# Half of the down projections' width as seven half-size products, and layer 1's attention on one folded block of keys

## The chip, the cores and the metric

The kernel runs on one core of a Trainium2 chip. The core has a matrix engine (PE, whose weight loads are listed as PEld), a vector engine (DVE), a scalar engine (ACT), a general engine (POOL), and a queue of its own for most DMA transfers (SP). They work beside each other and wait for each other through semaphores. SBUF is the core's working memory with 128 partitions; PSUM is the small memory that PE writes its sums to.

The metric is the time of one execution in microseconds, as the device measures it; the figure for a kernel is the median of several runs.

## The reference

One sequence of 512 tokens of width 1024 passes two layers. Layer 0 mixes the tokens with a gated delta rule, layer 1 with attention over a sliding window of 128 tokens; both add attention into 256 memory tokens, and both are followed by an MLP with 4096 hidden features.

```python
def sliding_window_sink_attention(q, k, v, sinks):
    ...
    s = jnp.einsum('bnqhgd,bnkhd->bnhgqk', qb, kk).astype(jnp.float32) * (dh ** -0.5)
    qi = jnp.arange(WINDOW)[:, None]
    kj = jnp.arange(2 * WINDOW)[None, :]
    diff = qi + WINDOW - kj
    band = (diff >= 0) & (diff < WINDOW)
    ...
    m = jnp.maximum(jnp.max(s, axis=-1, keepdims=True), sink)
    p = jnp.exp(s - m)
    denom = jnp.sum(p, axis=-1, keepdims=True) + jnp.exp(sink - m)
    probs = (p / denom).astype(v.dtype)
    o = jnp.einsum('bnhgqk,bnkhd->bnqhgd', probs, vv)

def sq_relu_mlp(h, w_up, w_down):
    return jnp.square(jax.nn.relu(h @ w_up)) @ w_down

    for layer in range(DEPTH):
        ...
        h = layer_norm(DN_ALPHA * h + mix, ln_g[layer, 0], ln_b[layer, 0])
        h = layer_norm(DN_ALPHA * h + sq_relu_mlp(h, mlp_w_up[layer], mlp_w_down[layer]),
                       ln_g[layer, 1], ln_b[layer, 1])
        if layer == N_A - 1:
            k_sh, v_sh = shared_kv(h, w_kv_shared, cos, sin)
```

With blocks of 128 tokens, a query sees key j of its own block where j is not after it, and key j of the block before where j is after it: for each j exactly one of the two.

## The kernel before

**Numbers.** Every large product is done with operands split in two: a high part, rounded to the form that PE multiplies quickly (float32r), and a low part, the rest. A product is three matmuls: high by high, high by low, low by high. `split` (L967) and `wload` (L102) make such a pair of tiles from a raw one (`wr`): ACT copies the high part (`wh`), DVE subtracts it from the raw tile (`wl`). `hidden` (L979) does the same to the hidden values after squaring them.

**The MLP** (`mlp`, L960 to L1233) goes through eight chunks of 512 hidden features. In one turn of the loop at L1198 the downs of chunk c stand beside the ups of chunk c + 1, in two sections, n = 0 and 1; with chunk 7 only downs are left (`downs_last`, L1157).

A section begins with the up products of a `Pair` (L1073): two blocks of 128 features, computed as a 2 x 2 block product with seven half-size products in place of eight, in the order m1, m6, m2, m7, m5, m4, m3. Each is 12 matmuls of 256 columns. The sums of tokens that this needs are made once per layer (`x_sums`). The sums of weights are made by POOL in `up_load` (L1052: four operations, from the raw tiles into `sa` and `sb`) and then split (`split0`, `split_b`, `split_a`, `split2`). The partial results are joined by DVE in `u2`, `u3` and the four quarters of `r`, which read PSUM; `close` applies ReLU and the square and splits the result.

Then come the downs of the section (`down`, L1138): for each of the four tiles of 128 tokens, twelve matmuls of 512 columns into one bank of PSUM (`mmt`, three banks in turn), which DVE adds to `res` (L1149). The weights are two slabs per section, by `dn_slab` (L1151). Between the four tiles the splits of the next section's pair are issued, so that they stand on ACT and DVE while PE works on the downs.

**Order.** PE's order is that of the program (`T`, a wrapper, chains each matmul to the one before where it matters). On the other engines the framework's scheduler may reorder; `behind(a, b)` puts a behind b without a wait. The gain and shift of the first layer norm are loaded by `load_gb` (L861) into a pool of their own before the MLP; those of the second at the end of chunk 1.

**Layer 1's mixer** runs the steps of LAYER1_ORDER (L41): w loads weights, k makes the shared keys and values, q the queries, a one `attend` (half of the heads, one tile of tokens), o an output projection, l a layer norm, and F empties the pipeline of units. `attend` pushes two units of four heads each. A unit has three stages, which are put between the other steps: `scores` (six matmuls per pair of heads over one or two blocks of keys; masked maximum by L1344; exponential by L1351; sink; scaling by L1362), `turn` (transposes of each 128 x 128 block of weights by PE into `spt`, copies to `pT`), and `values` (`ov`). Tile 0 has one block of keys, tiles 1 to 3 two. In half 1 the second unit is the memory's.

Of the kernel before, what the change touches and what calls it, by code (L numbers as in the profile page):

```python
# [18 lines left out]
P = 128  # L19
# [21 lines left out]
LAYER1_ORDER = """w2 k1 k2 w01 k0 k3 q11 q12 q10 a11 w00 q13 a10 q00 a13 a12 a00 q02 w10 q01 a01 a02 q03 w11 o00 a03 o01 F o02 o03  # L41
o11 o10 l1 o12 l0 o13 l2 l3"""
# [8 lines left out]
def trunk(ctx: ExitStack, tc: tile.TileContext, xT, xn, memT, wk, wq, wv, wqm, wz, wmk, wmv, wo0, wo1, up, dn,  # L51
# [38 lines left out]
    def mmt(n="mm"):  # L90
        return pmm.tile([P, 512], F32, tag="mm", name=nm(n))
# [769 lines left out]
    def load_gb(i):  # L861
        g_t = late[0].tile([P, D], F32, tag="lng", name=nm("lng"), bufs=1)
        b_t = late[0].tile([P, D], F32, tag="lnb", name=nm("lnb"), bufs=1)
        SY.dma_start(g_t, lng[i:i + 1, :].broadcast_to([P, D]))
        SY.dma_start(b_t, lnb[i:i + 1, :].broadcast_to([P, D]))
        return g_t, b_t
# [59 lines left out]
    gb0 = load_gb(0)  # L926
# [34 lines left out]
    def mlp(pool, layer, last, gb0):  # L961
# [5 lines left out]
        def f4(shape, n):  # L967
            return pool.tile(shape, F32, tag="f4", name=nm(n), bufs=5)
# [42 lines left out]
        def ups_second(hid):  # L1011

            for f in range(2):
# [3 lines left out]
                r = f4([P, 512], "relu")  # L1017
# [8 lines left out]
        def x_sums():  # L1026
# [5 lines left out]
            else:  # L1032
                f11, f12, f21, f22 = t1, *(f4([P, 4, HT], n) for n in ("f12", "f21", "f22"))
# [19 lines left out]
        def up_load(f, e):  # L1053
# [7 lines left out]
            e.tensor_tensor(sb[:, 1], raw[0][:, kB], sb[:, 0], op=ALU.subtract)  # L1061
            return raw, sa, sb
# [9 lines left out]
        class Pair:  # L1072


            def __init__(self, f0, e=G):
                self.f0 = f0
                self.raw, self.sa, self.sb = up_load(f0, e)

            def split0(self, first):
                hi, lo = split(self.raw[0], [P, KT, P], first=first)  # L1080
                self.A11, self.A12 = (hi[:, kA], lo[:, kA]), (hi[:, kB], lo[:, kB])

            def split_b(self):
                hi, lo = split(self.sb, [P, 2, 4, P])
                self.S2, self.S4 = ((hi[:, i], lo[:, i]) for i in range(2))

            def split_a(self, first=None):
                hi, lo = split(self.sa, [P, 2, 4, P], first=first)
                self.S1, self.S3 = ((hi[:, i], lo[:, i]) for i in range(2))

            def split2(self, first_act=None):
                self.A22 = split(self.raw[1][:, kB], [P, 4, P], "w2h", first_act=first_act)
# [16 lines left out]
            def m2(self):  # L1109
                product(self.a, self.A12, xq["B21"], False, True)  # L1110
                self.r = f4([P, 2, 512], "r")
                A.activation(self.r[:, 0, tA], self.a, AF.Relu)
# [11 lines left out]
            def m4(self):  # L1124
                product(self.b, self.A22, xq["T4"], False, True)
                V.tensor_tensor(self.r[:, 1, tA], self.s1, self.b, op=ALU.add)
# [29 lines left out]

        def downs_last(hid):  # L1157
# [27 lines left out]

        hid, nxt = ups_first()
        gb1 = done = None
        tables = rotary_tables(pool) if layer == 0 else None
        for c in range(NC - 1):
            later = new_hid()  # L1190
            for n in range(2):
                p, nxt = nxt, None
                f0 = 4 * c + 2 * n + 6
                early = c == n == 0
                if p is None:
                    ups_second(later)
                    slabs = dn_slabs(c, n)
                else:  # L1198
# [8 lines left out]
                    p.split2(None if early else done)  # L1207
                    slabs = [dn_slab(c, n, 0, p.u2_in, p.m1_out)] if early else dn_slabs(c, n)
# [5 lines left out]
                    p.m4()  # L1214
                    p.m3()
                    p.close(later)
                    done = p.last
                if layer == 0 and c == 0:
# [9 lines left out]
                down(c, 0, n, hid, slabs)  # L1228
                if nxt:
                    nxt.split0(p and p.r22)  # L1230
                down(c, 1, n, hid, slabs)
                if nxt:
                    nxt.split_b()  # L1233
                down(c, 2, n, hid, slabs)
                if nxt:
                    nxt.split_a()
                down(c, 3, n, hid, slabs)
            if c == 1:
# [255 lines left out]
```

## Time and profile before

| | |
|---|---|
| median of 3 runs | 1158.35 us (1158.11 to 1158.95) |
| the profiled execution | 1156.52 us |
| its span | 1154.8 us |
| layer 0's mixer | 0 to about 314 us |
| layer 0's MLP | about 314 to 655 us |
| layer 1's mixer | about 655 to 821 us |
| layer 1's MLP | about 821 us to the end |

The span reaches from the first to the last instruction of the trace; the execution's own time has 1.7 us around it. PE is busy 306.84 us of the first of these four stretches, 338.62 of the second and 326.08 of the last. Times from the trace are those of this one execution, and a row with a count (x12) covers that many instructions of one kind.

### The profile page before, as it was taken

Reading aid. Unit: us, or ns where it says so; the run is one execution under the profiler, and the core shown is the slowest. Engines: PE = TensorE matmul, PEld = TensorE weight load, DVE = VectorE, ACT = ScalarE, POOL = GpSimd, SP = SyncE. Lnnn points to the kernel's source line nnn. Section 1 sums busy time; section 2 is a strip of 40 time slices with the busy share of each in tenths; the row PEclk is TensorE's granted clock in tenths of the full one; section 3 lists DMA queues with packets and bytes.
Section 4 is the critical chain, followed back from the end, with each engine's and each line's share of the span. In section 5 each row is a group of like instructions: output and inputs, shape, how many; then the busy total and the mean of one; then the engine's idle time right before and its main releaser. Section 6 shows DMA issues by size and latency. Waiting matters only on the chain.

```text
span 1154.8 us, 19153 instructions
## 1 busy us (share of the span) xinstructions
PE 1135.5 (98%) x7578; PEld 1006.6 (87%) x7578; DVE 820.1 (71%) x1562; ACT 560.0 (48%) x1015; POOL 240.3 (21%) x172
## 2 busy tenths in 40 slices
PE   9999999999999999999999999999999999999997
PEld 9878789989998898998988887778988998989986
DVE  6667789767887676666665968886976665666657
ACT  6454843465584444454443336652645444444531
POOL 1112120011022242423320100000042432424203
PEclk9999999899999999999999999999999999999999
DMA  8522132304313243322334231102332332323311
GB/s 298 162 75 78 47 94 66 102 19 172 103 56 128 92 130 108 109 93 91 117 103 127 77 108 55 56 20 74 110 128 92 104 116 91 110 93 110 108 56 73
DMA packets 41258, 114.11 MB, mean 99 GB/s; under 512 B 11536, under 2 KB 12304, under 8 KB 41168
## 3 DMA queue, kind: packets, MB, share of 16 engines
q1 hardware_dynamic: 40736, 112.10, 29.9%
q8 instruction: 59, 0.97, 0.3%
q10 hardware_dynamic: 432, 0.79, 0.2%
q14 instruction: 31, 0.25, 0.1%
HBM read 109.46 MB, written 3.41 MB: 98 GB/s over the span
## 4 chain that ended last, share of the span: by engine, by line
PE 87%; DVE 6%; issue 2%; ACT 2%; POOL 1%; DMA 0%; DVEq 0%; ACTq 0%; POOLq 0%; SPq 0%
PE dn L69 30%; PE upb L69 9%; PE upd L69 6%; PE upa L69 6%; PE wo L69 5%; PE up L69 4%; PE kq L69 4%; PE projqMM L69 3%; PE proj_zMM L69 3%; PE v L69 3%; PE ov L69 1%; PE ssc L69 1%; DVE wl L109 1%; PE VM L69 1%; PE spt L72 1%
## 5 line engine op out<-in xcount | busy, mean ns | idle before, releaser
L108 ACT CAST wh<-wr 128x1024 fp32r<-128x1024 f32 (+1 forms) x124 | 130.5, 1053 | 218.8 <-PE dn L69 154.8
L109 DVE TENSOR_TENSOR wl<-wr,wh 128x1024 fp32r<-128x1024 f32 (+1 forms) x124 | 168.4, 1359 | 69.7 <-ACT wh L108 69.3
L69 PE MATMUL dn<-wh,hh 128*128 128x512 f32 (+1 forms) x516 | 200.2, 388 | 0.0
L69 PE MATMUL dn<-wh,hl 128*128 128x512 f32 (+1 forms) x516 | 200.1, 388 | 0.0
L69 PE MATMUL dn<-wl,hh 128*128 128x512 f32 (+1 forms) x516 | 200.1, 388 | 0.0
L1149 DVE TENSOR_TENSOR res<-res,dn 128x512 f32<-128x512 f32 (+1 forms) x121 | 82.1, 678 | 64.4 <-PE dn L69 64.3
L69 PEld LDWEIGHTS dn<-wh,hl 128*128 128x128 f32 x516 | 96.9, 188 | 19.9
L69 PEld LDWEIGHTS dn<-wh,hh 128*128 128x128 f32 x516 | 96.9, 188 | 18.9
L69 PEld LDWEIGHTS dn<-wl,hh 128*128 128x128 f32 x516 | 96.9, 188 | 18.9
L1058 POOL TENSOR_TENSOR sa<-wr 128x512 f32<-128x512 f32 x26 | 37.1, 1427 | 358.3 <-DMA wr<-in_up_dram 358.3
L825 POOL TENSOR_TENSOR rs<-rs,nhalf 128x1 f32<-128x1 f32 x16 | 13.0, 815 | 307.4 <-DVE rs L824 253.6
L69 PE MATMUL upb<-TH,wh 128*128 128x256 f32 x216 | 60.3, 279 | 0.0
L69 PE MATMUL upd<-XL,wh 128*128 128x256 f32 x216 | 59.8, 277 | 0.5 <-DVE XL L1204 0.5
L69 PE MATMUL upd<-XH,wh 128*128 128x256 f32 x216 | 59.8, 277 | 0.2 <-DVE r L1122 0.2
L69 PE MATMUL upa<-XL,wh 128*128 128x256 f32 x216 | 59.9, 277 | 0.0
L69 PE MATMUL upd<-XH,wl 128*128 128x256 f32 x216 | 59.7, 276 | 0.0
L69 PE MATMUL upa<-XH,wl 128*128 128x256 f32 x216 | 59.7, 276 | 0.0
L69 PE MATMUL upb<-TL,wh 128*128 128x256 f32 x216 | 59.7, 276 | 0.0
L69 PE MATMUL upb<-TH,wl 128*128 128x256 f32 x216 | 59.7, 276 | 0.0
L1060 POOL TENSOR_TENSOR sa<-wr,wr 128x512 f32<-128x512 f32 x26 | 59.1, 2272 | 0.0
L1059 POOL TENSOR_TENSOR sb<-sa,wr 128x512 f32<-128x512 f32 x26 | 54.7, 2104 | 0.0
L975 ACT CAST wh<-wr 128x1024 fp32r<-128x1024 f32 x27 | 28.5, 1054 | 53.6 <-PE upa L69 53.6
(414 smaller groups left out, 3253.5 us busy)
## 6 DMA issues: line engine op xcount, KB each, us to landing
wr<-in_up_dram SPq DMA_DIRECT2D x64, 512.0 KB, 3.7
wr<-in_dn_dram SPq DMA_DIRECT2D x64, 512.0 KB, 3.8
wr<-in_wo_dram SPq DMA_DIRECT2D x16, 512.0 KB, 4.1
wr<-in_bw_dram SPq DMA_DIRECT2D x8, 512.0 KB, 4.2
wr<-in_wk_dram SPq DMA_DIRECT2D x6, 512.0 KB, 4.3
wr<-in_wq_dram SPq DMA_DIRECT2D x6, 512.0 KB, 3.5
wr<-in_wv_dram SPq DMA_DIRECT2D x6, 512.0 KB, 3.5
wr<-in_wz_dram SPq DMA_DIRECT2D x4, 520.0 KB, 3.9
```

The lines of the kernel that those rows point to most:

```text
L69: return self.note(nc.tensor.matmul(*args, **kw))
L72: return self.note(nc.tensor.transpose(*args, **kw))
L108: behind(A.copy(hi, raw), first_act)
L109: behind(V.tensor_sub(lo, raw, fr(hi)), first)
L825: G.tensor_tensor(rs, rs, nhalf[:, 0:1], op=ALU.pow)
L975: behind(A.copy(hi, raw), first_act)
L1058: e.tensor_tensor(sa[:, 0], raw[1][:, kA], raw[1][:, kB], op=ALU.add)
L1059: e.tensor_tensor(sb[:, 0], sa[:, 0], raw[0][:, kA], op=ALU.subtract)
L1060: e.tensor_tensor(sa[:, 1], raw[0][:, kA], raw[1][:, kA], op=ALU.subtract)
L1149: V.tensor_tensor(dst, dst, ps, op=ALU.add)
```

## The change

**Downs.** For chunks 2 to 6 (`SD`) of both layers, the first 512 columns of the output are computed as before but in two parts of 256 (`Quarter`: eight tiles of 12 matmuls of 256 columns, weights loaded in parts of 256 columns). The second 512 columns are a 2 x 2 block product of 512 tokens by 512 features with 512 features by 512 columns, by seven products (`Down`; m1, m2 and m6 in section 0, m5, m7, m3 and m4 in section 1), each 12 matmuls of 256 columns into one bank of PSUM, two tiles of tokens beside each other. `a` (bank 0) gathers m1, m6, m7 and m4 and is added to its place in `res` after each of them; `d` (bank 1) gathers m5 and m3. POOL makes four sums of weights (`sums`, `sums_2`, `sums_3`) and four of hidden values (`Sums`, in place on `r`); the results are split by ACT and DVE. The banks of `mmt` get names. The splits of the next pair are put behind the last down product or tile issued and behind the hidden values. `f4` has three buffers in place of five; `r` gets three of its own, and `tb` and `S` are new tiles.

**Gain and shift.** Those of the first norm go to the memory of the tiles `S` (layer 0, loaded in `mlp`) or to layer 1's pool; those of the second are loaded at the end of chunk 6 into buffers of `f4`.

**Attention.** Units of tiles 1 to 3 that aren't the memory's fold the two blocks of scores into one: where a key of the own block is after the query, `copy_predicated` writes the score of the block before over it. Maximum, exponential and scaling then cover 128 keys in place of 256, and four blocks are transposed in place of eight. The values become all weights by the values of the block before, plus the weights of the own block (`cu`, masked by `own`) by the difference of the two blocks' values (`vstep`, by POOL). LAYER1_ORDER is another.

```diff
-LAYER1_ORDER = """w2 k1 k2 w01 k0 k3 q11 q12 q10 a11 w00 q13 a10 q00 a13 a12 a00 q02 w10 q01 a01 a02 q03 w11 o00 a03 o01 F o02 o03
-o11 o10 l1 o12 l0 o13 l2 l3"""
+LAYER1_ORDER = """w2 k1 k0 k2 w01 k3 q11 a11 w00 q10 q12 q13 a10 a12 q00 a00 q02 a13 w10 q01 a01 a02 q03 a03 w11 o00
+o01 o02 F o03 o11 o10 l1 o12 l0 l2 o13 l3"""
...
+    def mmt(n="mm", bank=None):
+        if bank is None:
+            bank = turn_of[0] % 3
+            turn_of[0] += 1
+        return pmm.tile([P, 512], F32, tag=f"mm{bank}", name=nm(n), bufs=1)
...
+            return pool.tile(shape, F32, tag="f4", name=nm(n), bufs=3)
+        def rt(shape, n):
+            return pool.tile(shape, F32, tag="r", name=nm(n), bufs=3)
+        def tb(n):
+            return pool.tile([P, 4, 256], F32, tag="tb", name=nm(n), bufs=1)
...
+        SD = range(2, NC - 1)
+        nA, nB = slice(512, 768), slice(768, 1024)
+        class Quarter:
+            def __init__(self, c, m):
+                self.c, self.m = c, m
+                self.raw = columns(c, 0, m)
+            def split(self, *first):
+                self.w = split(self.raw, [P, 4, 256], "wh", *first)
+            def tile(self, t, hid):
+                (hh, hl), (wh, wl) = hid, self.w
+                ps = smt("dnq")[:, 0:256]
+                for k in range(4):
+                    h, l = (x[:, k, t * P:(t + 1) * P] for x in hid)
+                    T.matmul(ps, h, wh[:, k, :], start=k == 0, stop=False)
+                    T.matmul(ps, h, wl[:, k, :], start=False, stop=False)
+                    T.matmul(ps, l, wh[:, k, :], start=False, stop=k == 3)
+                dst = res[:, t, self.m * 256:self.m * 256 + 256]
+                return V.tensor_tensor(dst, dst, ps, op=ALU.add)
...
+        def columns(c, n, m):
+            raw = wpool[0].tile([P, 4, 256], F32, tag="wr", name=nm("wr"), bufs=wpool[1])
+            for i in range(2):
+                SY.dma_start(raw[:, 2 * i:2 * i + 2, :], dn[layer, c, n, i][:, :, m * 256:m * 256 + 256])
+            return raw
+        class Down:
+            def __init__(self, c):
+                self.R0, self.R1 = (columns(c, 1, m) for m in range(2))
+                self.tb = tb("tb")
+            def sums(self, first):
+                b11, b21, b12, b22 = (r[:, i:i + 2, :] for r in (self.R0, self.R1) for i in (0, 2))
+                t3 = self.tb[:, 0:2, :]
+                behind(G.tensor_tensor(t3, b22, b12, op=ALU.subtract), first)
+                G.tensor_tensor(b12, b12, b11, op=ALU.subtract)
+            def sums_2(self):
+                t1, b22 = self.R1[:, 0:2, :], self.R1[:, 2:4, :]
+                G.tensor_tensor(self.R0[:, 0:2, :], b22, t1, op=ALU.subtract)
+            def sums_3(self, first):
+                behind(G.tensor_tensor(self.tb[:, 2:4, :], self.R0[:, 2:4, :], self.R0[:, 0:2, :], op=ALU.subtract),
+                       first)
...
+            def product(self, ps, h, f, t, w, start, stop, rows, cols):
+                (hh, hl), (wh, wl) = h, w
+                for j in range(2):
+                    tk = slice(t.start + j * P, t.start + j * P + P)
+                    for k in range(2):
+                        a, b = (x[:, f + k, tk] for x in h)
+                        T.matmul(ps[:, j, :], a, wh[:, k, :], start=start and j == 0 and k == 0, stop=False,
+                                 skip_group_check=True)
+                        T.matmul(ps[:, j, :], a, wl[:, k, :], start=False, stop=False, skip_group_check=True)
+                        T.matmul(ps[:, j, :], b, wh[:, k, :], start=False, stop=stop and k == 1, skip_group_check=True)
+                for rw, cl in zip(rows, cols):
+                    dst = res[:, rw.start // P:rw.stop // P, cl]
+                    self.out = V.tensor_tensor(dst, dst, ps, op=ALU.add)
...
+            def m1(self):
+                self.a = self.open(0)
+                self.product(self.a, self.hid, 0, tA, self.B11, True, False, [tA], [nA])
+            def m2(self):
+                self.product(self.open(1), self.hid, 2, tA, self.B21, True, True, [tA], [nA])
+            def m6(self):
+                self.product(self.a, self.s[0], 0, tA, self.T2, False, False, [tA], [nB])
+            def m5(self):
+                self.d = self.open(1)
+                self.product(self.d, self.s[1], 0, tB, self.T1, True, False, [tB], [nB])
+            def m7(self):
+                self.product(self.a, self.s[0], 0, tB, self.T3, False, False, [tB], [nB])
+            def m3(self):
+                self.product(self.d, self.s[1], 0, tA, self.B22, False, True, [tA], [nB])
+            def m4(self):
+                self.product(self.a, self.hid, 2, tB, self.T4, False, True, [tB], [nA])
...
+        class Sums:
+            def __init__(self, r0, r1):
+                self.r = r0, r1
+                a11, a21, a12, a22 = (r[:, :, t] for r in self.r for t in (tA, tB))
+                G.tensor_tensor(a22, a21, a22, op=ALU.add)
+                G.tensor_tensor(a21, a11, a21, op=ALU.subtract)
+                G.tensor_tensor(a11, a22, a11, op=ALU.subtract)
+                self.last = G.tensor_tensor(a12, a12, a11, op=ALU.subtract)
+            def split(self, i, first, first_act):
+                hi, lo = (pool.tile([P, 2, 512], F32R, tag=f"S{n}{i}", name=nm(f"S{n}{i}"), bufs=1) for n in "HL")
+                behind(A.copy(hi, self.r[i]), first_act)
+                behind(V.tensor_sub(lo, self.r[i], fr(hi)), first)
+                return hi, lo
...
+        if layer == 0:
+            gb0 = load_gb(0, *gbt)
...
+                if fast and n == 0:
+                    q = Quarter(c, 0)
+                    d = Down(c)
+                    d.hid = hid
+                    d.sums(s_.last)
...
+                    p.split2(None if early else done, p.u2_in if fast else None)
+                    if not fast:
+                        slabs = [dn_slab(c, n, 0, p.u2_in, p.m1_out)] if early else dn_slabs(c, n)
+                    elif n == 0:
+                        q.split(p.u2_in, p.m1_out)
+                    else:
+                        d.split_1(p.u2_in, p.m1_out)
...
+                    if fast and n == 0:
+                        d.split_0(p.u3_in, p.m2_out)
+                        d.sums_2()
+                    if fast and n == 1:
+                        q.split(p.u3_in, p.m2_out)
...
+                        d.split_t2(p.r22, p.m2_out)
+                        d.s = [s_.split(0, p.r22, p.m2_out)]
+                    if fast and n == 1:
+                        d.s.append(s_.split(1, p.r22, p.m2_out))
...
+                        d.split_2(p.r21, p.m2_out)
...
+                if n == 1 and c + 1 in SD:
+                    sums = Sums(rs_[0], rs_[1])
...
+                elif n == 0:
+                    d.sums_3(nxt.sums)
+                    q.tile(0, hid)
+                    d.m1()
+                    nxt.split0(d.out, p.last)
+                    q.tile(1, hid)
+                    d.m2()
+                    nxt.split_b(d.out, p.last)
+                    o = q.tile(2, hid)
+                    d.m6()
+                    nxt.split_a(o, p.last)
+                    q.tile(3, hid)
+                    q = Quarter(c, 1)
+                else:
+                    d.m5()
+                    if nxt:
+                        nxt.split0(d.out, p.last)
+                    q.tile(0, hid)
+                    d.m7()
+                    o = q.tile(1, hid)
+                    if nxt:
+                        nxt.split_b(o, p.last)
+                    d.m3()
+                    if nxt:
+                        nxt.split_a(d.out, p.last)
+                    q.tile(2, hid)
+                    q.tile(3, hid)
+                    d.m4()
+            s_ = sums
+            if c == NC - 2:
+                gb1 = load_gb(2 * layer + 1, *(f4([P, D], n) for n in ("lng", "lnb")))
...
+            if t not in vsteps:
+                vsteps[t] = lt([P, 2, 64], f"vstep{t}", 1)
+                G.tensor_tensor(vsteps[t], vS[:, t], vS[:, t - 1], op=ALU.subtract)
+            return vsteps[t]
...
+                    if fold:
+                        for r in range(2):
+                            V.copy_predicated(sc[r][:, :, P:], each(before, 2), sc[r][:, :, :P])
+                            sc[r] = sc[r][:, :, P:]
...
+                    if fold:
+                        V.tensor_tensor(pm[:, :, :P], pm[:, :, :P], den[:, :].unsqueeze(2).broadcast_to([P, 4, P]), op=ALU.mult)
...
+                def turn_fold():
+                    pt = smt("spt").rearrange("p (r j i) -> p r j i", r=2, j=2)
                     for r in range(2):
                         for j in range(2):
-                            h = 2 * j + r
-                            V.tensor_scalar(pm[:, h, :nk * P], pm[:, h, :nk * P], den[:, h:h + 1], None, op0=ALU.mult)
+                            T.transpose(pt[:, r, j, :], st["pm"][:, 2 * j + r, :P], ident)
+                    all_, cu = (lt([P, 2, 2, P], "pT", 6) for _ in range(2))
+                    flat = lambda x: x.rearrange("p r j i -> p (r j) i")
+                    A.copy(all_, pt)
+                    V.tensor_tensor(flat(cu), flat(pt), each(own, 4), op=ALU.mult)
+                    st["pT"] = [[x[:, r] for x in (all_, cu)] for r in range(2)]
...
+                                v = (VM1[:, b, js.start, r, :] if mem else vstep(t)[:, r, :] if fold and b
+                                     else vS[:, t - nb + 1 + b, r, :])
+                                T.matmul(ov[64 * r:64 * r + 64, js, :], v, pT[r][b][:, js, :], start=(b == 0),
                                          stop=(b == nk - 1))
```

More of the change, by code (lines that the diff above doesn't have):

```diff
@@ L859, in ln_tile, with load_gb @@
             V.tensor_sub(ls, hT, fr(hs))
-    def load_gb(i):
-        g_t = late[0].tile([P, D], F32, tag="lng", name=nm("lng"), bufs=1)
-        b_t = late[0].tile([P, D], F32, tag="lnb", name=nm("lnb"), bufs=1)
+    def load_gb(i, g_t, b_t):
         SY.dma_start(g_t, lng[i:i + 1, :].broadcast_to([P, D]))
@@ L959, in rotary_tables, with mlp @@
         yield
-    def mlp(pool, layer, last, gb0):
+    def mlp(pool, layer, last):
         NC = 8
@@ L1319, in unit @@
                 nk = 2 if mem else nb
+                fold = not mem and nb == 2
+                W = (2 if mem else 1) * P
                 h0 = half * 8 + 4 * q
@@ L1330, in scores @@
                             qh, ql = (x[rows, 2 * q + j, :] for x in qT)
[L1331 removed]
+                            kh, kl = (x[rows, j, :] for x in KM1) if mem else (x[rows, k0:k0 + nb * P] for x in kTs)
                             ops.append(((qh, kh), (qh, kl), (ql, kh)))
@@ L1390, in values @@
                     split_copy(ov, *((XH[:, k, tok(t)], XL[:, k, tok(t)]) if half == 0 else [x[:, k] for x in mixTs[t]]))
-                return scores, turn, values
+                return scores, turn_fold if fold else turn, values
             for q in range(2):
@@ L1412, in load_slabs @@
                 slabs["W", n[1]] = [wload(wo1[n[1], i], [P, 2, 512]) for i in range(4)]
-        gb0 = load_gb(2)
+        gb0 = load_gb(2, *(lt([P, D], n, 1) for n in ("lng", "lnb")))
         run_steps(LAYER1_ORDER, {"w": load_slabs, "k": shared_kv, "q": projq, "a": attend, "F": flush, "o": out1,
```

121 lines of the change are left out of this document (76 added, 45 removed).

## The prediction

> **What bounds the kernel now.** I read the page's busy shares first, then the chain of work that ended last, then one stretch of it, then the busy times by stretch.
>
> ```profile
> span 1154.8 us, 19153 instructions
> PE 1135.5 (98%) x7578; PEld 1006.6 (87%) x7578; DVE 820.1 (71%) x1562; ACT 560.0 (48%) x1015; POOL 240.3 (21%) x172
> ...
> PE 87%; DVE 6%; issue 2%; ACT 2%; POOL 1%; DMA 0%; DVEq 0%; ACTq 0%; POOLq 0%; SPq 0%
> ```
>
> PE is 87% of the chain. The next rows are one section of an MLP (seven half-size up products, then 48 down matmuls of 512 columns) and, behind them, busy times of such a section in layer 0 and of layer 1's mixer (columns: window and its us, then busy PE, PEld, DVE, ACT, POOL, granted clock, DMA share, GB/s).
>
> ```profile
> 443.66 1.38 PE upa L69 x12
> 445.04 1.36 PE upb L69 x12
> 446.40 1.36 PE upa L69 x12
> ...
> 453.20 10.89 PE dn L69 x48
> ```
>
> ```profile
> 443.70:464.10 20.40, 20.40 (x134) 18.52 (x133) 12.92 (x20) 9.39 (x11) 8.26 (x6) 1.00 0.31 104
> 654.80:821.00 166.20, 163.95 (x1058) 130.55 (x1057) 135.41 (x399) 81.76 (x229) 4.62 (x5) 1.00 0.22 72
> ```
>
> The section has no idle PE; DVE is busy 63% of it, POOL 40%. In the mixer PE lacks 2.25 us of 166.20. So fewer matmul columns shorten the kernel, as long as DVE, ACT and POOL, which get more to do, still come in time.
>
> **The change, part by part.** *Matmuls of the downs.* A chunk now has two sections of 48 matmuls of 512 columns. From chunk 2 to 6 it has eight quarter tiles of 12 matmuls of 256 columns (half the width) and seven products of 12 of 256. By the rows above 48 of 512 cost 10.89 (226.9 ns each) and 12 of 256 cost 1.36 (113.3 each), the same per column. So 2 x 10.89 = 21.78 becomes 15 x 1.36 = 20.40, 1.38 less per chunk. Two layers of five chunks: **-13.8 us**. This assumes that token-major matmuls of 256 columns run at the pitch of the ups, 113 ns.
>
> The Trainium skill, TensorE: Matmul & The Clock Gate, section Back-to-back issue gap, has N/2.4 + 2.5 ns, so that each matmul costs a fixed part and halving the columns is not free. By it a chunk would fall from 96 x 215.8 = 20.72 to 180 x 109.2 = 19.65, an estimate of -10.7 us in all; the rows show no fixed part (226.9 against 113.3), and the measurement decides.
>
> *The pitch can be another.*
>
> ```profile
> 484.52 1.38 PE upa L69 x12
> ...
> 488.62 1.48 PE upb L69 x12
> 490.10 1.41 PE upd L69 x12
> ```
>
> ```profile
> 654.81 5.65 PE ropeMM L69 x48
> ```
>
> ```profile
> 1144.16 0.28 PE L69 MATMUL dn<-wl,hh 128*128 128x256 f32 x1
> ...
> 1146.80 0.28 PE L69 MATMUL dn<-wh,hl 128*128 128x256 f32 x1
> ```
>
> After a short stall at 488.62 the same ups run at 1.41, 118 ns, until the 512-column downs; ropeMM, token-major, runs at 118; the last tile's 256-column downs run 22 pitches in 2.64 us, 120 ns. Fast chunks have no 512-column matmul that would end such a state; what else ends it is m1's first operand, a copy, with which all steady sections begin at 113. I take 113 because the streams enter the downs from ups at 113 with nothing between, and keep 120 as an end: 180 x 6.7 ns = 1.2 us per chunk.
>
> *DVE, ACT and POOL.* Columns of the groups: count, busy us, mean ns, idle before.
>
> ```profile
> L1149 DVE TENSOR_TENSOR res<-res,dn 128x512 f32<-128x512 f32 x119 | 81.2, 683 | 64.4 <-PE dn L69 64.3
> L1122 DVE TENSOR_TENSOR r<-u,upd 128x256 f32<-128x256 f32 x27 | 11.4, 421 | 23.0 <-PE upd L69 23.0
> L975 ACT CAST wh<-sa 128x1024 fp32r<-128x1024 f32 x27 | 28.3, 1050 | 39.9 <-PE upd L69 39.9
> ```
>
> ```profile
> 546.17 1.56 DVE L109 TENSOR_TENSOR wl<-wr,wh 128x1024 fp32r<-128x1024 f32 x1 [1.76 <-ACT wh L108]
> 547.65 0.68 DVE L1149 TENSOR_TENSOR res<-res,dn 128x512 f32<-128x512 f32 x1
> 548.25 1.74 DVE L109 TENSOR_TENSOR wl<-wr,wh 128x1024 fp32r<-128x1024 f32 x1
> ...
> 553.76 1.22 DVE L976 TENSOR_TENSOR wl<-wr,wh 128x1024 fp32r<-128x1024 f32 x1
> 554.89 0.41 DVE L1126 TENSOR_TENSOR r<-m,upb 128x256 f32<-128x256 f32 x1
> 555.23 1.22 DVE L976 TENSOR_TENSOR wl<-sb,wh 128x1024 fp32r<-128x1024 f32 x1
> ```
>
> ```profile
> 545.34 1.31 POOL L1058 TENSOR_TENSOR sa<-wr 128x512 f32<-128x512 f32 x1 [13.38 <-DMA wr<-in_up_dram]
> 546.61 2.30 POOL L1060 TENSOR_TENSOR sa<-wr,wr 128x512 f32<-128x512 f32 x1
> 548.87 2.28 POOL L1059 TENSOR_TENSOR sb<-sa,wr 128x512 f32<-128x512 f32 x1
> ```
>
> A split's subtraction (two operands in SBUF) takes 1.22 alone and 1.56 or 1.74 beside POOL; a POOL sum 1.31 alone and 2.30 beside it. Each waits for the whole of the other; adds from PSUM wait for nothing. One step from start to start: 1.13 (553.76 to 554.89), 0.34, about 0.60 for 512 columns, and 1.27 on POOL.
>
> A chunk's DVE work afterwards: 15 splits of 1024 columns (six of the two pairs, two of hidden values, seven new: two quarters, R0, R1, tb, two sums of hidden values) at 1.13 = 17.0; three of 512 at 0.60 = 1.8; 18 adds of 256 at 0.34 = 6.1; seven of 512 at 0.60 = 4.2. That is 29.1 of 39.5 us (19.1 ups, 20.4 downs), 74%. POOL goes from 8 to 16 sums (four Sums, four in Down): 20.3, 51%. ACT adds 3.5 casts of 1.05: 22.5, 57%. Cover exists, but what excludes each other, 18.8 + 20.3 = 39.1, is 99% of the chunk. Before, four sums cost DVE 0.34 + 0.52 = 0.86, 0.22 each; 16 give 3.4, and DVE 32.5 of 39.5 (82%).
>
> What is late next: u2, u3 and r22. Each PSUM tile is read one product (1.36) before PE writes it again; less about 0.3 to begin and 0.41, 0.65 is left, and a split of 1.22 that waits 1.2 for POOL ahead of the read overruns it. The added splits sit exactly there, queued on DVE behind u2, u3 and r22, and PE waits for what is behind them. In the downs the banks come back after three products and more (4 us), so the seven new adds are hidden. POOL's sums wait for loads and hidden values and fall mostly into the downs, those of Down into the first section's ups. No such section is in the trace; the nearest stall is 488.62's: 0.12, then 0.05 in each product. Ends: nothing, and rival 1's 45 us. I take 0.25 per section, twenty sections: **+5.0 us**.
>
> *Loads.* Down weights come as eight 256 KB loads in place of four of 512 KB, in runs of 1 KB; DMA is busy 31% (row above) and a raw tile has some 10 us: nothing. Gain and shift rows move. gb0 stands ahead of the up weights in the code and in memory that wo still reads at 313.94:
>
> ```profile
> 280.98 4.25 SPq L105 DMA_DIRECT2D wr<-in_up_dram  x4
> ...
> 323.24 0.33 SPq L864 DMA_DIRECT2D lng<-in_lng_dram  x1
> 335.25 0.89 SPq L1056 DMA_DIRECT2D wr<-in_up_dram  x2
> ```
>
> The load at 323.24 stands later in the code than the one at 335.25, so SP's order lets ready loads pass: nothing. Were SP to stand at it until 314, weights would land 3.7 later and be split by 320, where `up` now begins at 314.85: +5. gb1 goes to chunk 6, long before its use. Named PSUM banks and the smaller DMA scratch: nothing, no row against it.
>
> *Layer 1's attention.* Nine units (three tiles; two of half 0, one of half 1) turn four 128x128 blocks in place of eight.
>
> ```profile
> 750.50 0.87 PE spt L72 x8
> ```
>
> 36 x 0.109 = **-3.9 us**. Score and value matmuls stay. DVE per unit:
>
> ```profile
> L1362 DVE TENSOR_SCALAR pm<-pm,sden 128x256 f32<-128x256 f32 x52 | 14.8, 347 | 0.1
> L1344 DVE CUSTOM_DVE_ANT_0 pm<-ssc,band 128x256 f32<-128x256 f32 x36 | 13.2, 419 | 1.4 <-PE ssc L69 1.4
> L1351 ACT ACTIVATE pm<-pm,smx 128x256 f32<-128x256 f32 x36 | 17.9, 499 | 3.9 <-DVE smx L1347 3.5
> L1351 ACT ACTIVATE pm<-pm,smx 128x128 f32<-128x128 f32 x12 | 4.7, 392 | 0.6 <-DVE smx L1347 0.6
> ```
>
> Four masked maxima of 0.42 and four scalings of 0.35 (3.1) go; two predicated copies, two maxima (0.42 to 0.69 each) and one product (0.6) come, 2.3 to 3.4; the exponentials save 4 x 0.11. Beside PE this is nothing; the new order can win at most PE's missing 2.25 or lose as much: 0.
>
> **Sum:** -13.8 + 5.0 - 3.9 = -12.7. The profiled execution took 1156.52, with 1.7 around its span, 1.8 below the median of 1158.35; taken off both, 1143.8 and **1145.6 us**.
>
> **Rivals.** *1. DVE is the bound* (slower). If each of POOL's 16 sums holds DVE up by what a sum itself lost, 2.30 - 1.31 = 0.99, a chunk takes 29.1 + 15.8 = 45 us against 40.9: 10 x 4.1 - 3.9 = +37, 1195 us. It is slower from 0.76 per sum on. For it: 99%. Against it: 0.22 so far, and half of DVE's time needs nothing that POOL holds. 12%. The Trainium skill, SBUF — State Buffer, Who interferes with whom, calls this an exclusive lock on a shared port pair; the trace agrees (1.31 against 2.30), and that rule is what could make this rival come true.
>
> *2. The pitch falls to 120 in the downs:* +11.9, so -0.8, 1157.5 us. For it: every token-major stream of 256 columns in the trace; against it: no stall before them. With 118 (180 x 4.7 ns, +8.5) it is 1154. 23%, about a third of it within 0.2% of before.
>
> *3. Nothing late:* no stalls, and the mixer's idle gone: -13.8 - 3.9 - 2.25 = -20, 1138.4 us. 10%.
>
> **How the numbers follow.** The forecast (stalls between 0 and 0.5 per section, 1141 to 1151) 55%. Range: low 1138.4, high rival 2's 1157.5, as 1138 to 1158, with rival 1 left out. Measurement can tell 0.2%, 2.3 us. Faster 0.79, same 0.08, slower 0.13.
>
> **What would show it.** Right: chunks of about 40 us from chunk 2 on with 1.36 per product and tile; the ups' seven products a little over 1.36 where u3 and r22 wait; spt matmuls 116 down to 80. Wrong: products of 1.41 to 1.44 throughout (rival 2); wl subtractions near 2.3 and chunks over 41 (rival 1); up weights landing after 314 (SP stood still).

## The result and the profile after

The changed kernel is slower: 1177.01 us (1174.14 to 1178.09, 4 runs) against 1158.65 (1158.11 to 1159.58, 4 runs) of the kernel before measured beside it, ratio 1.0147 (95% interval 1.0130 to 1.0164). The forecast was 1145.6, its range ended at 1158. The profiled execution took 1177.97, its span is 1176.3.

The page of the changed kernel, its busy shares and its chain:

```profile
span 1176.3 us, 20996 instructions
PE 1145.3 (97%) x8382; PEld 1046.5 (89%) x8382; DVE 931.3 (79%) x1611; ACT 581.2 (49%) x1055; POOL 373.7 (32%) x257
...
PE 78%; DVE 11%; issue 4%; ACT 3%; POOL 2%; DMA 1%; SPq 0%; DVEq 0%; POOLq 0%; ACTq 0%
```

With fewer columns to multiply, PE is busy 9.8 us longer (1135.5 before), and DVE's share of the chain has gone from 6% to 11%. The chain through layer 1's first fast chunk (start, length, tile, number of matmuls; the fast chunks are 2 to 6, which have the new downs):

```profile
946.52 1.36 PE upd L69 x12
947.88 1.42 PE dnq L69 x12
949.30 1.44 PE dns L69 x12
...
956.50 1.44 PE dnq L69 x12
957.94 1.42 PE upa L69 x12
959.35 1.41 PE upb L69 x12
...
966.42 1.41 PE upd L69 x12
```

The pitch is the time from one matmul's start to the next. The ups enter at 113 ns (1.36 for twelve), the downs run at 120 (1.44), and the next ups carry on at 118 (1.41). Nothing waits here, so this is PE's own pace. Later chunks add waits. Two of them, by stretches (columns as in the prediction):

```profile
999.50:1041.30 41.80, 41.61 (x350) 41.19 (x349) 36.18 (x44) 21.50 (x26) 27.10 (x16) 1.00 0.31 101
1020.90:1062.80 41.90, 41.71 (x351) 41.28 (x350) 36.27 (x44) 21.49 (x26) 27.19 (x17) 1.00 0.32 102
```

Layer 1's later fast chunks take 41.7 to 41.9 and layer 0's 41.2 to 43.7, where the kernel before took 40.9 to 41.2 and the forecast had 40. The granted clock of these two is 1.00, so the clock is not their cause. By stages, from the first matmul of one kind to the first of the next in each trace:

| stage | before | after | difference |
|---|---|---|---|
| start to layer 0's first pair | 339.4 | 342.4 | +3.0 |
| layer 0's chunks 0 and 1 | 83.6 | 86.3 | +2.7 |
| layer 0's fast chunks and last downs | 229.2 | 235.3 | +6.1 |
| shared keys (first ropeMM to first projqMM) | 13.5 | 18.5 | +5.0 |
| rest of layer 1's mixer | 147.5 | 145.2 | -2.3 |
| layer 1's first ups and downs | 45.9 | 47.8 | +1.9 |
| layer 1's chunks 0 and 1 (from the first pair) | 61.3 | 62.7 | +1.4 |
| layer 1's fast chunks to the end | 234.4 | 238.1 | +3.7 |

Of the first row's 3.0, little belongs to the change: four runs below that leave this stage's code alone (e1, e4, e7 and e8) reach the MLP 0.9 to 2.9 us later than the profiled execution of before, which was a quick one. The granted clock differs there: from 200 to 300 us it averages 0.95 before and in e4 (+0.9), and 0.93 in the changed kernel, e1, e7 and e8 (+1.9 to +2.9).

### The profile page after: what moved, and what is told of

Its sections match the earlier page's. It is cut to its first block, busy times and chain, and to the rows that moved or that the text cites. A ratio compares the mean times of both kernels' runs of the same rounds, so it can differ in the third digit from the quotient of the medians.

```text
span 1176.3 us, 20996 instructions
## 1 busy us (share of the span) xinstructions
PE 1145.3 (97%) x8382; PEld 1046.5 (89%) x8382; DVE 931.3 (79%) x1611; ACT 581.2 (49%) x1055; POOL 373.7 (32%) x257
## 4 chain that ended last, share of the span: by engine, by line
PE 78%; DVE 11%; issue 4%; ACT 3%; POOL 2%; DMA 1%; SPq 0%; DVEq 0%; POOLq 0%; ACTq 0%
PE dn L69 10%; PE dnq L69 9%; PE upb L69 9%; PE dns L69 8%; PE upd L69 5%; PE wo L69 5%; PE upa L69 5%; PE projqMM L69 4%; PE kq L69 4%; PE proj_zMM L69 3%; PE v L69 3%; PE up L69 2%; PE ssc L69 1%; DVE wl L115 1%; PE ov L69 1%
## 5 line engine op out<-in xcount | busy, mean ns | idle before, releaser
L986 DVE TENSOR_TENSOR wl<-wr,wh 128x1024 fp32r<-128x1024 f32 x67 | 100.4, 1498 | 0.0
L69 PE MATMUL dnq<-wh,hh 128*128 128x256 f32 x320 | 90.5, 283 | 0.0
L69 PE MATMUL dnq<-wh,hl 128*128 128x256 f32 x320 | 90.5, 283 | 0.0
L69 PE MATMUL dnq<-wl,hh 128*128 128x256 f32 x320 | 90.5, 283 | 0.0
L69 PE MATMUL dn<-wh,hh 128*128 128x512 f32 (+1 forms) x196 | 75.9, 387 | 1.5 <-DVE res L1157 1.4
L69 PE MATMUL dn<-wh,hl 128*128 128x512 f32 (+1 forms) x196 | 75.6, 386 | 0.0
L69 PE MATMUL dn<-wl,hh 128*128 128x512 f32 (+1 forms) x196 | 75.5, 385 | 0.0
L69 PEld LDWEIGHTS dnq<-wh,hl 128*128 128x128 f32 x320 | 61.3, 192 | 0.0
L69 PEld LDWEIGHTS dnq<-wh,hh 128*128 128x128 f32 x320 | 61.3, 191 | 0.0
L69 PEld LDWEIGHTS dnq<-wl,hh 128*128 128x128 f32 x320 | 61.3, 191 | 0.0
```

The source lines that it names most:

```text
L69: return self.note(nc.tensor.matmul(*args, **kw))
L986: behind(V.tensor_sub(lo, raw, fr(hi)), first)
```

## The experiments

Ratios are to runs of the kernel before taken beside these on the same chip.

| run | median us | ratio (95%) |
|---|---|---|
| e1_256 | 1185.99 | 1.0225 (1.0208 to 1.0243) |
| e2_nosum | 1170.38 | 1.0093 (1.0075 to 1.0111) |
| e3_mlp | 1179.40 | 1.0176 (1.0156 to 1.0196) |
| e4_att | 1158.61 | 0.9986 (0.9972 to 1.0000) |
| e5_shift | 1179.29 | 1.0172 (1.0154 to 1.0191) |
| e6_half | 1183.79 | 1.0224 (1.0206 to 1.0242) |
| e7_gb | 1164.28 | 1.0049 (1.0034 to 1.0064) |
| e8_att_old | 1160.71 | 1.0015 (1.0005 to 1.0025) |
| e9_vs | 1176.93 | 1.0150 (1.0129 to 1.0171) |
| e10_kick | 1163.82 | one run |
| e11_pitch | 1170.88 | 1.0091 (1.0074 to 1.0108) |
| e12_pitch_nosum | 1150.84 | 0.9923 (0.9908 to 0.9938) |

### The width of the downs alone (e1)

```diff
-                down(c, 0, n, hid, slabs)
+                def downs(t):
+                    w = 256 if 2 <= c < NC - 1 else 512
+                    for i in range(0, 512, w):
+                        down(c, t, n, hid, slabs, slice(i, i + w))
+                downs(0)
```

> The kernel before, with the downs of chunks 2 to 6 as two parts of 256 columns in place of one of 512: same arithmetic, same splits, no added sum on POOL; only DVE has 16 adds of 256 per chunk for 8 of 512. Theory (the pitch): token-major matmuls of 256 columns run at 120 ns whatever the other engines do, and the ups behind them at 118 in place of 113. A chunk's downs then take 192 x 120 = 23.0 us in place of 21.8, its ups 0.7 more: 10 x 2 = +20 us, about 1178. Rival (the pitch is only what late operands leave behind, the loss is DVE's and POOL's): the downs run at 113, 1158 to 1160.

The kernel before, cut into 256 columns and otherwise untouched, loses 26 us, 6 more than the theory's 20. Its chain:

```profile
1014.50 11.51 PE dn L69 x96
1026.01 1.42 PE upa L69 x12
1027.42 1.41 PE upb L69 x12
```

96 matmuls in 11.51 are 120 ns each, against 10.89 for the same columns as 48. The ups behind them begin at 118, and in 11 of 18 sections a wait sets them back to 113. Such waits (at 1030.29 one product takes 1.63) come on top of the theory's price. So the pitch needs neither the added sums nor late operands; the rival falls.

### The sums left out (e2)

```diff
-                behind(G.tensor_tensor(t3, b22, b12, op=ALU.subtract), first)
-                G.tensor_tensor(b12, b12, b11, op=ALU.subtract)
...
-                G.tensor_tensor(a22, a21, a22, op=ALU.add)
-                G.tensor_tensor(a21, a11, a21, op=ALU.subtract)
```

(and so for the other four; the tile `tb` is loaded in their place)

> The changed kernel without the eight added sums on POOL per fast chunk; the parts that they would have made are read as they are, or loaded in place of being summed. Left out: the sums of weights and of hidden values of the down products. Theory (the pitch): downs stay at 1.44 per product and ups at 1.41; only the waits inside the ups go, some 0.4 to 0.9 per section: 1177 falls to about 1165 to 1172. Rival (DVE and POOL hold each other up, and the pitch follows from it): sections fall to 19.1 to 20 us, the whole to 1150 or less.

6.6 us go, and a chunk without any wait still takes more than before the change:

```profile
993.10:1034.40 41.30, 41.30 (x350) 41.30 (x349) 32.11 (x44) 21.48 (x26) 13.29 (x8) 1.00 0.37 116
```

PE is busy all of 41.30. From first up to first up such a chunk takes 41.38, its two sections 19.97 and 21.41: 15 products of 1.44 and 14 of 1.41. So the pitch alone turns -1.4 per chunk into about +0.5, and the waits behind the sums add the rest. The theory held, in its time too.

### Where the operands lie (e5), and tiles of 512 columns (e6)

```diff
+        late[0].tile([P, 48], F32, tag="pad7", name="pad7")
...
-        pool.tile([P, 16], F32, tag="pad5", name=nm("pad5"), bufs=1)
+        pool.tile([P, 32], F32, tag="pad5", name=nm("pad5"), bufs=1)
```

> The changed kernel with the hidden values and their sums (the downs' stationary operands) 192 bytes further, by pads alone: their addresses then stand at 32 modulo 256 in place of 224, while the down weights (moving) stay at 224. In the traces the streams of 256 columns with both at one residue run at 120 ns, those with residues 64 apart at 113 to 118. Theory (the pitch depends on how the two addresses stand): the fast chunks' downs run at 113 to 118, 0.03 to 0.08 less per product, 5 to 12 us in all, while the 512-column downs of chunks 0, 1 and 7 become slower by 4 to 8 ns per matmul (+2 to 5 us): 1167 to 1174, with products of 1.36 to 1.42. Rival (a token-major stream of 256 columns runs at 120 wherever it lies): products stay at 1.44 and the time at 1176 to 1180.

A residue here is what is left of an operand's address in SBUF modulo 256 bytes; the addresses are those of the compiled program. The chain at the place of the block shown above for the changed kernel:

```profile
944.72 1.36 PE upd L69 x12
946.08 1.41 PE dnq L69 x12
...
955.98 1.42 PE upa L69 x12
```

With the pads, every down product takes 1.41 in place of 1.44 (in sections without a wait) and each 512-column section 11.19 in place of 10.89. So the pitch does depend on how the two addresses stand. But the time is not the theory's: a chunk still takes 41.8, as the waits in the ups grew by what PE won. This was the first sign of a second bound close behind the first.

```diff
-                self.raw = columns(c, 0, m)
+                self.raw = wpool[0].tile([P, 2, 512], F32, tag="wr", name=nm("wr"), bufs=wpool[1])
+                SY.dma_start(self.raw, dn[layer, c, 0, m])
...
-                ps = smt("dnq")[:, 0:256]
-                for k in range(4):
+                ps = smt("dnq")
+                for k in range(2):
```

> The changed kernel with its first half of the output in tiles of 512 columns and half of the hidden features in place of 256 columns and all of them: the same eight tiles per chunk, six matmuls of 512 each, the same weights and splits, but eight adds of 512 on DVE for eight of 256 (+0.26 each). Theory (pitch of 256 columns): each such tile takes 1.36 in place of 1.44, and what follows a tile of 512 columns starts at 113 again; 8 x 0.08 = 0.64 per chunk, and perhaps 0.4 in section 1's ups, which follow such a tile: 1167 to 1172. Rival (DVE is the bound, and 2.1 us more of it per chunk shows): 1180 or more.

Here the rival's time was right. The wide tiles take 1.39 and some ups behind them start at 1.36 again, but with 2.1 us more of DVE's adds per chunk the kernel is 6.8 us slower than the changed one (1183.79 less 1177.01, not measured beside each other), and layer 1's fast chunks take 41.1 to 42.9. That it is these adds fits, but wasn't tried alone.

### Which first operand sets the pitch (e10)

```diff
+            o = OFFS[i % 8]
+            y = ytile[:, o:o + HT]
+            A.copy(y, fr(w))
...
-                    q.tile(0, hid)
+                    q.tile(0, hid, yk)
```

> The run without the added sums, with the downs' stationary operands at residue 32 as in the shifted run, and with copies as first moving operands at eight different residues in turn: in layer 1 for the first down matmul of every fast section, in both layers for the first up matmul of the section behind it. Left out: the sums, as in the run without them. Theory (with the sums gone PE sets the pace, and its pitch is a state, 113 or 118, that a stream keeps and that a single odd matmul at its head can set): without any kick a chunk takes 29 products of 1.41 = 41.0; some residues start the downs or the ups at 113 and they stay there, 1.36 per product, down to 39.5 per chunk. Rival (118 is the pitch of two alternating weight and operand streams and no first operand changes it): all products at 1.41 to 1.42 behind a fast section. Chunks over 41.2 would speak for a third limit that is neither the sums nor the pitch.

Both pitches occur, and each lasts until the next boundary. The chain over one such boundary:

```profile
983.00 1.41 PE dnq L69 x12
...
988.66 1.42 PE dnq L69 x12
990.07 1.37 PE upa L69 x12
991.44 1.36 PE upb L69 x12
...
998.24 1.36 PE upd L69 x12
999.60 1.38 PE dns L69 x12
1000.98 1.36 PE dnq L69 x12
```

For the downs, residues 64, 160 and 192 gave 113 (and 224, which is no odd operand at all, behind ups at 118), while 0, 32, 96 and 128 gave 118. Without an odd operand (layer 0) the downs ran at 113 in four of six sections behind ups at 118, and in none of four behind ups at 113. For the ups, 224 gave 113 behind either pitch; 0, 96 and 192 behind 118 (192 not behind 113); 32, 64, 128 and 160 never. Most of these were seen once or twice, many behind one pitch alone.

### The pitch mended, with and without the sums (e11, e12)

```diff
-                    q.tile(0, hid)
+                    q.tile(0, hid, yk)
+                    xq["first"] = copy_at(0, XH[:, 0, tA])
...
-                gb1 = load_gb(2 * layer + 1, *(f4([P, D], n) for n in ("lng", "lnb")))
+                gb1 = load_gb(2 * layer + 1, *(h[:, 0:2, :].rearrange("p a b -> p (a b)") for h in hid_tiles(F32)))
```

> The changed kernel, complete, with three mends: the downs' stationary operands at residue 32; copies as first moving operands at the two residues that gave 113 in the run before (64 for the first down matmul of a fast section, 224 for the first up matmul behind it); and the second norm's rows in the buffers of the hidden values that chunk 6 leaves, so that the MLP's pool ends earlier. Theory (with the pitch at 113, DVE and POOL are the bound of a fast chunk, since the shifted run won 0.03 per product on PE and nothing in the chunk): fast chunks stay at 41.4 to 41.9, the waits inside the ups grow; the stretch of the shared keys goes from 18.5 to about 14; the 512-column downs cost 0.3 more per section: 1170 to 1175. Rival (PE's pitch alone is the bound): fast chunks of 39.8 to 40.4, 1155 to 1163.

> The same without the eight added sums per fast chunk (left out as before). Theory and rival alike expect PE to set the pace here: 29 products of 1.36 plus what the first operands cost, 39.5 to 39.8 per chunk, 1147 to 1156. Were the chunks over 40.5, the first operands that gave 113 in turn would not do it side by side.

A chunk without sums (e12) and one with them (e11), by stretches:

```profile
999.80:1039.30 39.50, 39.50 (x351) 39.50 (x350) 32.15 (x44) 22.97 (x30) 13.12 (x8) 1.00 0.39 125
```

```profile
1016.90:1058.20 41.30, 40.34 (x349) 39.87 (x349) 36.34 (x44) 23.05 (x30) 28.52 (x16) 1.00 0.34 107
```

Without sums, PE takes the 39.5 us of matmuls that the prediction had counted. With them, 41.3, and the chain runs through DVE:

```profile
1034.60 2.34 DVE wl L987
1036.94 0.33 DVE res L1194
1037.27 0.60 DVE res L1255
1037.87 1.15 DVE wl L987
1039.02 0.04 issue
1039.06 1.45 PE upb L69 x10
```

DVE is 4.2 us busier than in e12 with the same 44 instructions: its two-operand subtractions wait for POOL's sums (2.34 for one of 1.22). It is not idle when PE wants it, but late. Per added sum that is 0.52, between the prediction's 0.22 and rival 1's 0.99. The sums cost 20.0 us here (1170.88 less 1150.84; 18.8 in the MLPs of the two profiled executions) and 6.6 us in the changed kernel (1177.01 less 1170.38; 7.9 when each is taken against its own runs of the kernel before), where the slower PE hid some two thirds of that.

### The attention and the rows of gain and shift (e3, e4, e8, e7, e9)

e3 undoes the change's attention and order; e4 makes only these; e8 is e4 with the old order (no diffs: they are parts of the change's own).

> The change without its attention: layer 1's attention and the order of its steps as before. Theory: the attention's part gave nothing back, since the first steps of layer 1's mixer lost about 5 us to the new order (the copies of the values and the rotary sums stand behind the last tile's layer norm on ACT and DVE) and the rest won about 1.5; this run's mixer is 3 to 5 us shorter than the changed kernel's and the whole 1172 to 1175. Rival (the loss in the mixer comes from the named PSUM banks or from the MLP, and the fold saves its 4 us): 1179 to 1181.

> The kernel before with the attention's part of the change alone (the fold and the new order of steps). Theory (the order's first steps cost more than the fold saves): layer 1's mixer 2 to 4 us longer than before, 1160 to 1163. Rival (the fold saves what was forecast and the loss comes from the rest): about 3.9 less, 1154 to 1155.

> The kernel before with the fold of the attention and the old order of steps. The fold with the new order has won 1.3 us of the 3.9 of the 36 transposes. Theory (the transposes saved are partly replaced by PE's waits for the longer chain on DVE, whatever the order): 1157.5 to 1160. Rival (the new order costs what is missing): 1154 to 1156.

e3's theory fell: the shared keys took 18.9 there with the old order too, so the loss isn't the attention's. e4 met neither of its forecasts: the fold with its new order wins 1.3 us alone (against 1159.89 beside it), and 2.4 in the change (1179.40 less 1177.01, not measured beside each other). With the old order it loses 1.3 (1160.71 against 1159.45 beside it), just past e8's theory, whose rival falls. The mixer from the first query matmul on, before and in e4:

```profile
665.70:813.20 147.50, 145.39 (x902) 112.40 (x900) 116.71 (x362) 72.93 (x211) 2.77 (x3) 1.00 0.18 58
```

```profile
667.70:813.10 145.40, 143.92 (x865) 109.57 (x864) 113.51 (x300) 68.73 (x211) 4.12 (x4) 1.00 0.18 62
```

36 transposes fewer, and 2.1 us in place of 3.9. From start to start, the transposes took 13.9 before and 9.1 in e4; but the same query and output matmuls took 1.1 more each and the scores 0.8. What makes these longer wasn't tried.

```diff
-                gb1 = load_gb(2 * layer + 1)
+                gb1 = load_gb(2 * layer + 1, *(f4([P, D], n) for n in ("lng", "lnb")))
...
-        gb0 = load_gb(2)
+        gb0 = load_gb(2, *(lt([P, D], n, 1) for n in ("lng", "lnb")))
```

> The kernel before with the gain and shift rows alone moved, as in the change: those of each layer's second norm into the MLP's rotating buffers at the end of chunk 6, those of layer 1's first norm into its mixer's pool. The run without the attention's part had the same 18.9 us from the first shared-key matmul to the first query matmul (13.5 before), so the attention isn't the cause. Theory (the shared values' tile lies where the second norm's rows lie, so its copies wait for the last tile's norm, and the rotary sums and PE behind them): that stretch becomes 17 to 19 us here too, about +5, 1163 to 1165. Rival (the named PSUM banks hold PE there): 13.5, 1158 to 1160.

Moving the rows alone costs 0.5%, and the stretch of the shared keys becomes 17.7. The first copy of the values on ACT, before, in the changed kernel and in e11, 4, 11 and 4 us behind the first ropeMM (652.2, 664.0 and 665.7):

```profile
656.26 0.27 ACT L1279 COPY vS<-ropeMM 128x128 f32<-128x128 f32 x1
```

```profile
674.64 0.27 ACT L1481 COPY vS<-ropeMM 128x128 f32<-128x128 f32 x1
```

```profile
669.62 0.27 ACT L1489 COPY vS<-ropeMM 128x128 f32<-128x128 f32 x1 [0.83 <-PE ropeMM L69]
```

On DVE, the last tile's norm read the rows until 674.0:

```profile
672.60 1.41 DVE L893 SCALAR_TENSOR_TENSOR res<-res,rs,lnb 128x512 f32<-128x512 f32 x2
```

```diff
-        vS = lt([P, NT, 2, 64], "vS", 1)
+        mixTs = [[lt([P, 4, P], f"mix{n}{t}", 1, F32R) for n in "hl"] for t in range(NT)]
+        vS = lt([P, NT, 2, 64], "vS", 1)
```

> The changed kernel with one tile of layer 1's pool placed elsewhere: the shared values now lie behind the eight tiles of the mixer's output and so no longer where the second norm's rows lie; nothing else differs. Theory (the 5 us between the first shared-key matmul and the first query matmul are ACT's copies of the values, which wait until the last tile's norm has read its rows): that stretch falls from 18.5 to 13.5 to 14.5, 1172 to 1174. Rival (another tile or the rows' load holds PE there): 17.5 or more, 1176 to 1178.

This theory fell in its detail: with the values' tile elsewhere the stretch still took 18.0. In the compiled program the first copy waits for PE alone before, and in the changed kernel and in e9 for that last instruction of the norm: the wait goes with the MLP's pool, out of which layer 1's pool is cut, not with one tile. e11 has the rows in the pool of the hidden values; its first copy waits for PE, and the stretch takes 13.6.

Not all of the 5.0 is PE standing still. In the changed kernel PE is busy 15.50 of the stretch's 18.5 us, before all of its 13.5: the granted clock averages 0.91 over it, 1.00 before and in e11. In e5, with the rows moved too, it stays at 1.00, and the stretch takes 17.3.

## Why the prediction was wrong

**The pitch.** The step that failed is "I take 113 because the streams enter the downs from ups at 113 with nothing between". The downs take no pitch over from the ups: it depends on where their two operands lie, and with both at one residue modulo 256 every stream of 256 columns in these traces runs at about 120. The quoted rows showed it (1144.16 to 1146.80, "120 ns"), and the prediction kept it as an end. Nor did "m1's first operand, a copy" end the state: the changed kernel's ups begin with it and carry on at 118. Rival 2 at 23% was the right mechanism, with two thirds of its price: its +11.9 left out these ups. Both together are about 18.8 us (41.38 in e2's chunk, less 39.5, ten times). (Its "every token-major stream" says too much: the prediction's own ropeMM row is one at 118.) The count of columns itself was right: e12 runs at 39.5.

The Trainium skill, SBUF — State Buffer, section Who interferes with whom, has PE reading its moving operand and its weights through independent ports. The runs show that the two still are not independent in the time that they take: pads alone, which moved one operand to another residue, took the pitch from 120 to 118 (e5). Whether the ports have a part in that, no run shows. The gap of N/2.4 + 2.5 that the prediction took from the Trainium skill, TensorE: Matmul & The Clock Gate, section Back-to-back issue gap, which gives it for an isolated matmul (109.2 for 256, an estimate), appears in no stream here; 113 is the lowest.

**DVE and POOL.** "+5.0" was measured as 6.6 to 7.9, but that holds only beside the slower PE; at the pitch that the prediction assumed it is about 20. So this term failed too, and that it came near 6.6 is luck. Rival 1 named the mechanism and put a chunk at 45; it is 41.3 (e11).

**The rows.** "gb1 goes to chunk 6, long before its use" looked at the load alone. What cost 5.0 us was how long the memory stays in use.

**The attention.** -3.9 became -1.3 to -2.4: the transposes went, and other matmuls took part of their time. That the new order can win or lose some 2 us against the old was right: e4 and e8 differ by 2.1, and by 2.5 against the kernel before beside each.

**Not foreseen, and partly open.** Chunks 0 and 1 of both layers lost 2.7 and 1.4 us. The wait is u2's; the changed kernel's timeline in such a section, first on DVE, then on POOL:

```profile
385.75 2.24 DVE L115 TENSOR_TENSOR wl<-wr,wh 128x1024 fp32r<-128x1024 f32 x1 [1.76 <-ACT wh L114]
...
388.51 1.72 DVE L115 TENSOR_TENSOR wl<-wr,wh 128x1024 fp32r<-128x1024 f32 x1
390.15 0.41 DVE L1117 TENSOR_TENSOR u<-m,upb 128x256 f32<-128x256 f32 x1
```

```profile
384.31 1.31 POOL L1068 TENSOR_TENSOR sa<-wr 128x512 f32<-128x512 f32 x1 [12.80 <-DMA wr<-in_up_dram]
385.58 1.32 POOL L1070 TENSOR_TENSOR sa<-wr,wr 128x512 f32<-128x512 f32 x1
386.86 2.29 POOL L1069 TENSOR_TENSOR sb<-sa,wr 128x512 f32<-128x512 f32 x1
```

POOL's second sum began 0.17 ahead of DVE's subtraction, which then took 2.24; at the same place before, the subtraction began at 382.13, 0.23 ahead of the sum, and took 1.36. e1, which leaves these chunks' code alone, lost 1.3 and 2.1 there too, so the code of the new downs isn't needed for it, and a small shift in time may decide it; which one was not tried. Layer 1's first ups lost 1.9 in every run with the change's MLP: POOL's first sum for the next pair stood beside DVE's unbroken row of two-operand work,

```profile
849.55 9.39 POOL L1068 TENSOR_TENSOR sa<-wr 128x512 f32<-128x512 f32 x1 [15.34 <-DVE TL L156]
```

and the pair's last sum ended at 862.85. ACT's cast of it waited for that, and the ReLU of the layer's first ups stood behind the cast:

```profile
862.89 1.05 ACT L985 CAST wh<-sb 128x1024 fp32r<-128x1024 f32 x1 [7.85 <-POOL sb L1071]
863.84 0.59 ACT L1028 ACTIVATE relu<-up 128x512 f32<-128x512 f32 x1
```

Before and in e7 these ReLUs stand ahead of the cast (before, at 848.37 and 850.19), and e7, with 7.20 for the same sum, lost nothing. So the held-off sum alone costs nothing there; behind it in the change's order on ACT, PE comes late. No run changed that order alone.

Added up, these come near to what separates forecast and measurement. The kernel was to win 12.7 and lost 18.4 against the runs beside it, 31.1 us apart; 18.8 (pitch), 1.6 (sums), 5.0 (rows), 1.5 (attention), 4.1 (chunks 0 and 1) and 1.9 (first ups) make 32.9. The sizes come from different pairs of runs, so they need not meet exactly.

No version with the full arithmetic is clearly faster than the kernel before. The attention alone (e4) comes nearest, 0.9986 with an interval that reaches 1.0000.

## What to carry to other kernels

Before counting columns, look up the pitch that the same kind of stream has in the trace, stationary and moving operand at the same relative addresses, and what the stream behind it inherits. Two engines that exclude each other can set the pace even when each has slack (DVE is busy 36.34 of e11's 41.30), and a faster PE uncovers what a slower one hid. For a buffer that moves, ask not only when it is filled but which pool it keeps open and what is cut out of that memory next.

## What the runs showed of the hardware

At a granted clock of 1.00 the matmul pitch of the MLPs takes one of a few values, each like a state that a stream keeps: 256 columns of float32r run at 113, 118 or 120 ns, the downs of 512 columns at 227 or 233 (10.89 or 11.19 for 48). Both operands at one residue modulo 256 (by the addresses in the compiled program) gave 120 and 227; residues 64 apart gave 113 or 118, and, in e5, 233. Within the latter, a first moving operand at another residue sets which of the two a stream keeps, for the 84 or 96 matmuls to the next boundary (e10, e12); a wait can change it on the way. A sum of two operands on POOL that takes 1.31 alone took 9.39 beside a row of DVE's two-operand instructions.
